# Feed-forward output projections as seven half-size products, with weight sums by accumulating DMAs, in a two-layer GLA and DeltaNet trunk

## The chip, the cores and the metric

The kernel runs on one core of one Trainium2 chip. The metric is the device time of one execution in microseconds (us); before the change it is 1276.69 us, the median of three runs (1276.61 to 1277.08). Engines are named as in the profile: PE is the tensor engine for matmuls, PEld its weight load, DVE the vector engine, ACT the scalar engine, POOL GpSimd, SP the engine that only issues DMAs. A DMA can be issued by SP or ACT through a hardware queue, or by POOL through a software queue.

## What is computed

The input x has 512 tokens of 1024 features in float32. Layer 0 mixes tokens with gated linear attention (GLA), layer 1 with gated DeltaNet (GDN). Each mixer and each feed-forward part is followed by a layer norm over the residual. Cut to what matters here:

```
def conv_ffn(x, w_in, conv_w, w_out):              # D_FF = 2816
    h = causal_dwconv(x @ w_in, conv_w)            # width 3, per channel
    gate, up = jnp.split(h, 2, axis=-1)
    return (jax.nn.gelu(gate, approximate=False) * up) @ w_out

for i in range(DEPTH):                             # DEPTH = 2
    y = gla_mixer(h, ...) if i % 3 == 0 else gdn_mixer(h, ...)
    h = layer_norm(ALPHA * h + y, ln_g[i, 0], ln_b[i, 0])
    h = layer_norm(ALPHA * h + conv_ffn(h, ...), ln_g[i, 1], ln_b[i, 1])
```

The change is in the last product of conv_ffn, (512 x 2816) times (2816 x 1024), once in each layer.

## The kernel before

**Precision.** Each float32 operand is split in two float32r parts, high and low: `split_out` (L450) lets ACT copy the source into the high part and DVE subtract it from the source for the low part. A product is three matmuls, high times high, high times low and low times high (`tm_terms`, L362, and `fm_mms`, L304).

**Two forms of product.** "fm" items (`fm_items`, L339) make 128 output features for all 512 tokens: the weights are held in the array, the tokens (`xh`, `xl`) stream, 8 blocks x 3 terms = 24 matmuls with 512 columns. "tm" products (`tm_half`, L367) make 128 tokens x 512 output columns: the activations are held and the weights stream.

**A feed-forward part** (`ffn`, L719) handles its 22 blocks of 128 inner features in two chunks of 12 and 10 (`CHUNKS`). For each block a gate item and an up item run; `ffn_conv` (L710) applies the three taps (one ACT pass, two DVE passes), ACT the GELU, DVE the product with the gate, and `split_out` makes `gh` and `gl`. Then `out_proj` (L403) multiplies the chunk with its rows of w_out: two column halves x four token blocks, each summed in a bank of PSUM over the chunk, then added to the residual h by DVE (L412 for the first chunk, L414 after it). In the last chunk the last four pairs of weight blocks (`TAIL`) are held in slots and the token blocks are finished one after another, with bn_stats (L419) and the layer norm spawned for each: `ln` (L606) between layers, which also makes the next `xh` and `xl` through PE transposes, or `ln_out` (L652) at the end, which stores the result. After a norm the first four fm items (`HEADSTART`) run first for tokens 0 to 255, then for 256 to 511, so that they begin before the last two blocks are normalised.

**Weights.** All weight tiles stand in one plan in the order of use. `issue` (L221) reads a tile of 512 KB by a DMA on SP into one of three raw buffers (`RAWB`) and splits it into one of four pairs of buffers (`WB`); `prefetch` (L285) issues up to `look` tiles ahead, 2 as a rule, while fewer than four are held. 

**Order.** Instructions are recorded by Python code that keeps a planned clock (`clk`) and runs side tasks as generators (`spawn`, `pump`); a scheduler then sets the final order on each engine. Every engine and every queue works through its own order, and a waiting instruction holds those behind it. Semaphores order the engines among each other.

**Memory.** All working tiles of 128 x 512 float32 come from one pool of 53 slots (`SLOTS`), the residual h among them. After the first feed-forward part h is written to DRAM by POOL's DMAs (`hd`) and read back after the GDN core (`unspill`, L671).

Of the kernel before, what the change touches and what calls it, by code (L numbers as in the profile page):

```python
# [25 lines left out]
ALPHA = 4.0 ** 0.25  # L26
LN_EPS = 1e-5
# [3 lines left out]
CHUNKS = ((0, 12), (12, 22))  # L31
SLOTS = 53
# [16 lines left out]
def blk(i, n=P):  # L49
    return slice(i * n, i * n + n)  # L50


class Trunk:
# [3 lines left out]
    def __init__(self, ctx, tc):  # L57
        self.tc = tc
        self.nc = nc = tc.nc
        self.n = 0  # L60
        ec = ctx.enter_context
        ap = ec(tc.tile_pool(name="acts", bufs=1))
        self.xh = ap.tile([P, NC, S], F32R, name="xh", tag="xh")
        self.xl = ap.tile([P, NC, S], F32R, name="xl", tag="xl")
        self.wp = ec(tc.tile_pool(name="wts", bufs=WB))
        self.mp = ec(tc.tile_pool(name="mem", bufs=SLOTS))
# [4 lines left out]
        self.dp = ec(tc.tile_pool(name="scratch", bufs=1, space=bass.MemoryType.DRAM))  # L71
        self.ident = self.keep([P, P], "ident")
# [5 lines left out]
        self.reset = self.keep([P, S], "reset")  # L78
        nc.vector.memset(self.reset, 1.0)
        nc.vector.memset(c4(self.reset)[:, :, 0:1], 0.0)  # L80
        self.h = None
        self.plan = []
        self.issued = 0
        self.taken = 0
# [12 lines left out]
        self.late = []  # L97
        self.first = None
        self.between = None
# [5 lines left out]

    def slot(self, s, dt=F32):
        return self.mp.tile([P, S], dt, name=self.uid(s), tag="slot")
# [4 lines left out]
    def small(self, shape, s, dt=F32, bufs=None):  # L112
        return self.sp.tile(shape, dt, name=self.uid(s), tag=s, bufs=bufs)

# [41 lines left out]
    def mm(self, out, a, b, start=True, stop=True):  # L156
# [4 lines left out]
        t = self.nc.tensor.matmul(out, a, b, start=start, stop=stop)  # L161
# [54 lines left out]

    @staticmethod
    def in_slots(item):
        return item[0] == "tm" and item[5]

    def issue(self, item):  # L221

        nc = self.nc
        if item[0] == "rep":
            return self.issue_rep(*item[1:])
        raw = self.rp.tile([P, 1024], F32, name=self.uid("raw"), tag="raw")
# [57 lines left out]

    def prefetch(self):  # L285
        while self.issued < min(len(self.plan), self.taken + self.look):
            item = self.plan[self.issued]
# [3 lines left out]
            self.issued += 1  # L291

# [46 lines left out]
    def fm_items(self, items):  # L339

        start = 0 if all(self.is_set(("x", tb)) for tb in range(NTB)) else HEADSTART
        first = items[:start]
        ws, banks = [], []
        for half in range(2 if first else 0):
            self.wait(("x", 2 * half), ("x", 2 * half + 1))
            for i, f in enumerate(first):
                if not half:
                    ws.append(self.weight())
                    banks.append(self.psum("fm"))
                self.fm_mms(banks[i], ws[i], half * 256, half * 256 + 256, self.pin and not half and i < 2)  # L350
                if half:
# [10 lines left out]
    def tm_terms(self, ps, ah, al, wh, wl, first, last):  # L362
        self.mm(ps, ah, wh, first, False)
        self.mm(ps, ah, wl, False, False)
        self.mm(ps, al, wh, False, last)
# [137 lines left out]
    def load_x(self, x):  # L503

        nc = self.nc
        self.h = [[self.slot("h") for _ in range(2)] for _ in range(NTB)]
# [99 lines left out]
    def ln(self, tb, spill=False):  # L606
# [36 lines left out]
        yield from self.until(("x", NTB - 1))  # L643
# [8 lines left out]
    def ln_out(self, tb, out):  # L652
        nc = self.nc
        gb, h = self.ln_gb(), self.h[tb]

        def center(mv):
            for hf in range(2):
                nc.vector.scalar_tensor_tensor(h[hf], h[hf], mv[:, 0:1], gb[hf], ALU.subtract, ALU.mult)

        mv, rs = self.ln_stats(tb, center)  # L660
        for hf in range(2):
            m = 2 if tb == NTB - 1 and hf else 1
            for i in range(m):
                cols = blk(i, S // m)
                nc.vector.scalar_tensor_tensor(h[hf][:, cols], h[hf][:, cols], rs, gb[2 + hf][:, cols],
                                               ALU.mult, ALU.add)
                (nc.sync, nc.scalar)[i].dma_start(out[blk(tb), hf * S + cols.start:hf * S + cols.stop],
                                                  h[hf][:, cols])
        yield 0.0

    def unspill(self, gb_rows):  # L671
# [4 lines left out]
        for hf in range(2):  # L676
            for tb in range(NTB):
                t = self.slot("h")
                nc.gpsimd.dma_start(t, self.hd[blk(tb), blk(hf, S)])
# [16 lines left out]
    def ffn_plan(self, w_in, w_out):  # L696
        for f0, f1 in CHUNKS:
# [3 lines left out]
            self.plan_out(w_out, f0 * P, f1 - f0, TAIL if f1 == NF else 0)  # L701
# [8 lines left out]
    def ffn_conv(self, ps, cw, b):  # L710
        nc = self.nc
        a = self.slot("conv")
# [6 lines left out]
    def ffn(self, cw, li, g, b, final, out=False):  # L719
        nc = self.nc  # L720
        for ci, (f0, f1) in enumerate(CHUNKS):
            gs, act, items = [], {}, []
            for f in range(f0, f1):
                def gate(ps, f=f):
                    a = self.ffn_conv(ps, cw, f)
# [3 lines left out]
                def up(ps, f=f):  # L729
                    u = self.ffn_conv(ps, cw, NF + f)  # L730
                    nc.vector.tensor_mul(u, u, act.pop(f))  # L731
                    t = self.slot("gh", F32R), self.slot("gl", F32R)
                    self.split_out(*t, u)
                    gs.append(t)
# [3 lines left out]
            last = ci == len(CHUNKS) - 1  # L738
# [5 lines left out]
            a = lambda c, tb: (gs[c][0][:, blk(tb)], gs[c][1][:, blk(tb)])  # L744
            self.out_proj(a, f1 - f0, ci == 0, final if last else None, 2 if last and out else 1)
# [38 lines left out]
    def gla_consts(self, w_gk2, b_gk, norm_w):  # L784
        nc = self.nc

        self.gk2 = self.keep([96, S], "gk2", F32R)
# [13 lines left out]
        self.gla_nw = self.keep([P, 256], "gla_nw")  # L801
# [8 lines left out]
        self.gla_mask = self.keep([P, S], "gla_mask", U8)  # L810
        nc.gpsimd.tensor_copy(self.gla_mask, mk)
        self.b_gk = self.keep([P, 4], "gla_b")
        self.spawn(self.columns([(b_gk.rearrange("(n p) -> n p", p=P), 4, self.b_gk)]), 12.0)

    def gla(self, li, g, b):
# [83 lines left out]
        ss = self.keep([P, GH, 4], "gla_ss")  # L899
        rr = self.keep([P, GH, 4], "gla_rr")  # L900
# [89 lines left out]
    def mixer_out(self, y, li, g, b, final=None):  # L990
# [7 lines left out]
        self.out_proj(a, NC, True, self.ln)  # L998

# [24 lines left out]
    def gdn_conv(self, ps, b):  # L1024

        nc = self.nc
        a = self.slot("conv")
# [8 lines left out]
    def gdn(self, li, g, b):  # L1036
        nc = self.nc
        self.flags = {f: t for f, t in self.flags.items() if f[0] in ("x", "h")}
        hs = slice(H0, H0 + 8)
        al = self.gdn_al  # L1040
        spilled = self.gb_rows
        keep = lambda s: self.keep([P, DH, 4], s)
        eb, neb, ebl, cd = (keep(s) for s in ("gd_eb", "gd_neb", "gd_ebl", "gd_cd"))
        bn, bp, rk = keep("gd_bn"), keep("gd_bp"), keep("gd_rk")
        ssq, rr = self.keep([P, 2, DH, 4], "gd_ssq"), self.keep([P, DH, 4], "gd_rr")
        bt = self.keep([P, 4, 64], "gd_bt")
# [7 lines left out]
        def ba_done(ps):  # L1054
# [8 lines left out]
            ea = self.keep([P, 1], "gd_ea")  # L1063
# [50 lines left out]
        def k_done(ps, hd):  # L1114
            k[hd] = self.gdn_conv(ps, 8 + hd)
# [4 lines left out]
        def q_done(ps, hd):  # L1120
            q[hd] = self.gdn_conv(ps, hd)
# [134 lines left out]
        def v_done(ps, hd):  # L1256
            vc[hd % 2] = self.gdn_conv(ps, 16 + hd)
# [145 lines left out]
def kernel(  # L1403
# [41 lines left out]
    t.drain()  # L1445

# [28 lines left out]
```

## Time and profile before

| | |
|---|---|
| median of three runs | 1276.69 us |
| span of the profiled execution, first to last instruction | 1274.8 us |
| time around the span, the difference of the two | 1.9 us |
| granted PE clock over the span | 0.999 |
| DMA queue of SP and its like (q1): moved, share of 16 engines | 116.28 MB, 31.1% |
| DMA queue of POOL (q0): moved, share of 16 engines | 8.50 MB, 2.3% |

The profiled execution is given by its span; its own time from launch to end isn't shown apart, so the runs' median is taken for it. In a row of instruction groups stand line, engine, operation, out<-in, shapes and count, then busy us and mean ns of one, then the idle time before them and who ended it. Busy times of one engine can overlap a little, since a matmul starts before the one ahead of it has drained. In a row of waits stand the waiting engine and line, the releaser, then us in total, times and the longest. In a piece of the chain or of the timeline stand start and length in us, engine, line and count. In a stretch, busy us and count of each engine are followed by the granted clock, the share of the 16 DMA engines that is busy, and GB/s.

### The profile page before, as it was taken

How to read it: one execution, taken by the hardware profiler on the slowest of the kernel's cores; microseconds unless marked ns; L12 is line 12 of the kernel's file. 1: busy time of each engine (PE TensorE's matmuls, PEld its weight loads, DVE VectorE, ACT ScalarE, POOL GpSimd, SP SyncE). 2: the span in 40 equal slices, each digit the busy share in tenths (PEclk: the TensorE clock that was granted, in tenths of full speed). 3: DMA queues.
4: the chain of work that ended last, by engine and by line, in shares of the span. 5: the costliest groups of instructions: out<-in, count | busy, mean ns of one | idle time of the engine just before them, and what ended most of it. 6: DMA issues, size and time to landing. Idle time of an engine off the chain costs nothing.

```text
span 1274.8 us, 17225 instructions
## 1 busy us (share of the span) xinstructions
PE 1260.9 (99%) x6682; PEld 1068.4 (84%) x6682; DVE 785.5 (62%) x1383; ACT 552.2 (43%) x1042; POOL 112.5 (9%) x152
## 2 busy tenths in 40 slices
PE   8999999999999999999999999999999999999997
PEld 8878888988888888889888888988988888888886
DVE  4953556676643466555789955679587653366656
ACT  4644444544421244435765544543644431244430
POOL 4000000070000000001023120100053000000000
PEclk9999999999999999999999999999999999999999
DMA  7322224143333333351354431234053333333331
GB/s 207 112 70 63 67 93 123 50 132 99 99 99 99 99 92 92 98 151 66 103 149 113 122 75 51 68 116 137 17 152 101 94 96 99 99 99 99 94 105 66
DMA packets 167234, 126.53 MB, mean 99 GB/s; under 512 B 16104, under 2 KB 139818, under 8 KB 167152
## 3 DMA queue, kind: packets, MB, share of 16 engines
q1 hardware_dynamic: 162064, 116.28, 31.1%
q0 software_dynamic: 3888, 8.50, 2.3%
q8 instruction: 52, 0.85, 0.3%
q10 hardware_dynamic: 1200, 0.66, 0.2%
q14 instruction: 30, 0.25, 0.1%
HBM read 119.63 MB, written 5.78 MB: 98 GB/s over the span
## 4 chain that ended last, share of the span: by engine, by line
PE 94%; DVE 3%; ACT 1%; DMA 1%; issue 1%; SPq 0%; DVEq 0%; ACTq 0%
PE fm L161 50%; PE tm L161 35%; PE o L161 2%; PE xT L178 1%; PE R L161 1%; PE V L161 1%; DVE wl L451 1%; PE qkT L178 1%; PE vn L161 1%; PE pq L161 1%; PE pg L161 1%; PE yT L178 1%; PE s L161 0%; DMA h<-in_x_dram 0%; PE qs L161 0%
## 5 line engine op out<-in xcount | busy, mean ns | idle before, releaser
L451 DVE TENSOR_TENSOR wl<-raw,wh 128x1024 fp32r<-128x1024 f32 (+1 forms) x190 | 237.8, 1253 | 312.2 <-ACT wh L451 312.0
L161 PE MATMUL fm<-xh,wh 128*128 128x512 f32 (+2 forms) x1104 | 402.6, 367 | 0.7 <-ACT xh L451 0.7
L161 PE MATMUL fm<-xl,wh 128*128 128x512 f32 (+2 forms) x1104 | 399.9, 365 | 0.0
L161 PE MATMUL fm<-xh,wl 128*128 128x512 f32 (+1 forms) x1088 | 396.0, 366 | 0.0
L451 ACT CAST wh<-raw 128x1024 fp32r<-128x1024 f32 (+1 forms) x190 | 199.0, 1047 | 279.4 <-PE tm L161 166.8
L161 PEld LDWEIGHTS fm<-xh,wh 128*128 128x128 f32 (+1 forms) x1104 | 206.9, 188 | 33.7 <-ACT xh L451 0.9
L161 PEld LDWEIGHTS fm<-xl,wh 128*128 128x128 f32 (+1 forms) x1104 | 207.0, 188 | 32.4
L161 PEld LDWEIGHTS fm<-xh,wl 128*128 128x128 f32 x1088 | 204.2, 189 | 33.5
L716 DVE SCALAR_TENSOR_TENSOR conv<-fm,ffn_cw,conv 128x511 f32<-128x511 f32 (+1 forms) x176 | 130.8, 746 | 3.0
L161 PE MATMUL tm<-wl,gh 128*128 128x512 f32 x290 | 112.4, 388 | 0.0
L161 PE MATMUL tm<-wh,gl 128*128 128x512 f32 x290 | 112.4, 388 | 0.0
L161 PE MATMUL tm<-wh,gh 128*128 128x512 f32 x290 | 112.4, 388 | 0.0
L451 ACT CAST gh<-conv 128x512 fp32r<-128x512 f32 x44 | 27.3, 621 | 124.2 <-DVE conv L731 124.1
L161 PE MATMUL tm<-wh,xh 128*128 128x512 f32 x192 | 78.5, 409 | 0.8 <-ACT qk L836 0.8
L161 PE MATMUL tm<-wh,xl 128*128 128x512 f32 x192 | 75.2, 392 | 0.0
L161 PE MATMUL tm<-wl,xh 128*128 128x512 f32 x192 | 75.0, 390 | 0.0
L726 ACT ACTIVATE conv<-conv 128x512 f32<-128x512 f32 x44 | 27.8, 632 | 94.8 <-DVE conv L716 94.8
L161 PEld LDWEIGHTS tm<-wh,gl 128*128 128x128 f32 x290 | 54.4, 188 | 11.2
L161 PEld LDWEIGHTS tm<-wl,gh 128*128 128x128 f32 x290 | 54.4, 188 | 11.2
L161 PEld LDWEIGHTS tm<-wh,gh 128*128 128x128 f32 x290 | 54.4, 188 | 11.1
L714 ACT ACTIVATE conv<-fm,ffn_cw 128x512 f32<-128x512 f32 x88 | 60.0, 682 | 0.2
L647 POOL TENSOR_TENSOR h<-h,gb 128x512 f32<-128x512 f32 x16 | 27.1, 1716 | 344.3 <-DMA gb<-in_ln_g_dram 235.8
(280 smaller groups left out, 1556.5 us busy)
## 6 DMA issues: line engine op xcount, KB each, us to landing
raw<-in_ffn_w_in_dram SPq DMA_DIRECT2D x88, 512.0 KB, 3.8
raw<-in_ffn_w_out_dram SPq DMA_DIRECT2D x44, 512.0 KB, 3.8
raw<-in_gdn_w_in_dram SPq DMA_DIRECT2D x32, 512.0 KB, 4.0
raw<-in_gla_w_in_dram SPq DMA_DIRECT2D x23, 512.0 KB, 3.6
raw<-in_gla_w_out_dram SPq DMA_DIRECT2D x8, 512.0 KB, 3.7
raw<-in_gdn_w_out_dram SPq DMA_DIRECT2D x8, 512.0 KB, 3.8
h<-in_x_dram SPq DMA_DIRECT2D x8, 256.0 KB, 4.3
hd<-h POOLq DMA_DIRECT2D x8, 256.0 KB, 2.5
```

Of the source, the lines that this page charges most:

```text
L161: t = self.nc.tensor.matmul(out, a, b, start=start, stop=stop)
L178: t = self.nc.tensor.transpose(out, a, self.ident[:n, :n])
L451: return self.nc.scalar.copy(dst_h, src), self.nc.vector.tensor_sub(dst_l, src, dst_h)
L647: nc.gpsimd.tensor_mul(h[hf], h[hf], gb[hf])
L714: nc.scalar.activation(a, ps, AF.Identity, scale=tap(2))
L716: nc.vector.scalar_tensor_tensor(a[:, d:], ps[:, :S - d], tap(2 - d), a[:, d:], ALU.mult, ALU.add)
L726: nc.scalar.activation(a, a, AF.Gelu)
```

## The change

**Seven products.** With tokens in halves 1 and 2, pairs of inner feature blocks (even, odd) and output columns in halves, the output product is a 2 x 2 block product. In place of eight half-size products it is made of seven. `folded` replaces `out_proj` for the feed-forward parts; the mixers keep `out_proj`.

```
+FORMS = ("a11", "a22", "a12", "w1", "v2", "v3", "v4")
+FOLD = (("b11", "a11", 0), ("b21", "a12", 1), ("t1", "w1", 2), ("t2", "v2", 0), ("b22", "v4", 2), ("t3", "v3", 0),
+        ("t4", "a22", 0))
+NEXT = {"b11": "b12", "t1": "b22", "t2": "b21"}
-CHUNKS = ((0, 12), (12, 22))
-SLOTS = 53
+GROUPS = ((0, 8), (8, 16), (16, 22))
+SLOTS = 45
+FFN_SLOTS = 6
+FOLDED = 2
+PASSING = 4
+AHEAD = 2
```

Each entry of FOLD is a product: a weight quarter or sum, an activation form, and one of three pairs of PSUM banks. Products that share a pair go on summing in the same banks, and after each of them DVE adds or subtracts the banks' present value to one or another block of h:

```
+        banks = [[self.psum("fold") for _ in range(2)] for _ in range(3)]
...
+            at, op = {"b11": (top, ALU.add), "t1": (high, ALU.add), "t2": (right, ALU.subtract), "b21": (top, ALU.add),
+                      "t3": (high, ALU.subtract), "b22": (right, ALU.add), "t4": (low, ALU.add)}[name]
...
+        for name, form, at in FOLD:
+            f = FORMS.index(form) * 256
+            for i in range(0, m, 2):
+                w = self.weight()
+                n = min(2, m - i)
+                for r in range(2):
+                    ps = banks[at][r]
+                    for j in range(n):
+                        _, fh, fl = forms[i + j]
...
+                        self.tm_terms(ps, fh[:, cols], fl[:, cols], *w[j], begin, end, True)
+                    if i + 2 >= m:
+                        update(name, r, ps)
```

Here m is the number of pairs in a group, 4, 4 and 3; top and right are token blocks 2 and 3, high and low are blocks 0 and 1. A weight tile holds the quarters of two pairs (one in the last tile of a group of 3 pairs).

**Activation forms.** The up product of the even and the odd block of a pair is written into one tile; DVE makes four more 256-column parts, and `split_out` makes 1792 columns at once (in parts for the last pair of a group):

```
+                    nc.vector.tensor_sub(part(4), part(0), part(2))
+                    nc.vector.tensor_sub(part(5), part(4), part(1))
+                    nc.vector.tensor_sub(part(6), part(1), part(0))
+                    nc.vector.tensor_add(part(7), part(5), part(3))
```

**Weight sums.** Quarters b11, b21, b22 and b12 are read by SP into tiles of their own (`sum`, 2 buffers, and `pass`, 4 buffers), up to `AHEAD` beyond the prefetch. b11 becomes t1 = b11+b12, then t2 = t1+b22, then t4 = t2+b21 in place, and the tile of t3 is b12+b22. Each sum is an accumulating DMA on POOL's queue, recorded right after the split of the former value:

```
+        if add:
+            self.nc.gpsimd.dma_start(dst, src, accum_op=ALU.add)
+        else:
+            self.nc.sync.dma_start(dst, src)
...
+        self.fold_read(group, {"t3": "b12"}.get(name, name), i, t)
+        if name == "t3":
+            self.fold_read(group, "b22", i, t, True)
...
+        self.split_out(wh[:, cols], wl[:, cols], t[:, cols])
+        self.vec(0.62 * n)
+        if name in NEXT:
+            self.fold_read(group, NEXT[name], i, t, True)
```

In a fold `look` is 3 in place of 2.

**Pools by stage.** `stage` releases the pool of working tiles and opens a new one for the GLA mixer (45 slots), the first feed-forward part (6 slots beside the tiles above), the GDN mixer and the second feed-forward part. Constants of one mixer move from the constant pool into the stage's pool (`own`), the scan mask `reset` is set anew for the GDN mixer, and h gets a pool of 8 tiles of its own, which the GDN mixer uses for its eight k tiles while h is in DRAM.

**Ends.** In the last group h is complete first for token blocks 2 and 3, then for 0 and 1, and the norms are spawned in that order. The first fm items after it run for tokens 256 to 511 first:

```
+        self.halves = (0, 1)
-        for half in range(2 if first else 0):
+        for turn, half in enumerate(self.halves if first else ()):
...
+        if last:
+            self.halves = (1, 0)
```

In `ln_out` the last store that is cut in two is that of token block 1 in place of block 3.

More of the change, by code (lines that the diff above doesn't have):

```diff
@@ L83, in __init__ @@
         self.issued = 0
+        self.loaded = 0
         self.taken = 0
@@ L104, in uid, with stage, resets, resid @@
         return f"{s}_{self.n}"
+    def stage(self, name, slots):
+        if self.mp is not None:
+            self.mp.release()
+        self.mp = self.tc.alloc_tile_pool(name=name, bufs=slots, reuse_waits="tile")
+    def resets(self):
+        self.reset = self.own([P, S], "reset")
+        self.nc.vector.memset(self.reset, 1.0)
+        self.nc.vector.memset(c4(self.reset)[:, :, 0:1], 0.0)
+    def resid(self, s):
+        return self.hp.tile([P, S], F32, name=self.uid(s), tag="h")
     def slot(self, s, dt=F32):
@@ L160, in mm @@
         self.clk += n * (0.00045 if b.dtype == F32R else 0.00175)
-        t = self.nc.tensor.matmul(out, a, b, start=start, stop=stop)
+        t = self.nc.tensor.matmul(out, a, b, start=start, stop=stop, skip_group_check=joined)
         if self.pin:
@@ L215, in plan_out, with plan_fold @@
                 self.plan_tm(w, row + 2 * cp * P, min(2, n - 2 * cp), hf * S, hf == 1 and cp >= npair - tail)
+    def plan_fold(self, w, f0, f1):
+        group = {"w": w, "f0": f0, "m": (f1 - f0) // 2}
+        for name, _, _ in FOLD:
+            for i in range(0, group["m"], 2):
+                self.plan.append(("fold", group, name, i))
     @staticmethod
@@ L291, in prefetch, with load_ahead @@
             self.issued += 1
+        self.load_ahead(self.taken + self.look + AHEAD)
+    def load_ahead(self, until):
+        self.loaded = max(self.loaded, self.issued)
+        while self.loaded < min(len(self.plan), until) and self.plan[self.loaded][0] == "fold":
+            self.fold_load(*self.plan[self.loaded][1:])
+            self.loaded += 1
     def weight(self):
@@ L642, in ln @@
             return
-        yield from self.until(("x", NTB - 1))
+        for i in range(NTB):
+            yield from self.until(("x", i))
         yield RESID_DELAY + 10.0 * tb
@@ L661, in ln_out @@
         for hf in range(2):
-            m = 2 if tb == NTB - 1 and hf else 1
+            m = 2 if tb == 1 and hf else 1
             for i in range(m):
@@ L785, in gla_consts @@
         nc = self.nc
-        self.gk2 = self.keep([96, S], "gk2", F32R)
+        self.gk2 = self.own([96, S], "gk2", F32R)
         def factor():
@@ L800, in gla_consts @@
         self.spawn(factor(), 3.0)
-        self.gla_nw = self.keep([P, 256], "gla_nw")
+        self.gla_nw = self.own([P, 256], "gla_nw")
         self.late.append((self.gla_nw, norm_w))
```

167 lines of the change are left out of this document (125 added, 42 removed).

## The prediction

> **What bounds the kernel now.** I read the page first (busy shares, then the chain that ended last), then what the tensor engine waited for, then stretches.
>
> ```profile
> span 1274.8 us, 17225 instructions
> PE 1260.9 (99%) x6682; PEld 1068.4 (84%) x6682; DVE 785.5 (62%) x1383; ACT 552.2 (43%) x1042; POOL 112.5 (9%) x152
> PE 94%; DVE 3%; ACT 1%; DMA 1%; issue 1%; SPq 0%; DVEq 0%; ACTq 0%
> ```
> ```profile
> PE xT L178 <- DVE ln_mv L592: 1.0, 1, 1.0
> ```
> ```profile
> 1037.75 65.28 PE tm L161 x288
> 1103.03 108.80 PE fm L161 x480
> 1211.83 54.82 PE tm L161 x270
> ```
> ```profile
> core 0: us, PE busy (x) PEld busy (x) DVE busy (x) ACT busy (x) POOL busy (x), PEclk, DMA share, GB/s
> 300.00:365.00 65.00, 65.00 (x288) 53.84 (x287) 40.06 (x49) 26.73 (x37) 0.00 (x0) 1.00 0.33 98
> 370.00:424.00 54.00, 54.00 (x240) 44.69 (x239) 16.71 (x17) 10.55 (x10) 0.00 (x0) 1.00 0.32 95
> ```
>
> The chain is 94% PE, and PE is never held at a layer norm for more than the 1.0 us shown. The three chain pieces are the second feed-forward layer from its first output product on; PE runs through them without a gap. So a matmul that goes is time saved, unless PE begins to wait. One 128x512 matmul costs 65.28/288 = 0.2267 us (a row of its own says 0.39 because neighbours overlap). The stretches show the room beside PE at full clock: DVE is busy 62% while the up-projections run and 31% during the output product; the DMA engines are busy 0.32 at 95 GB/s, so all 16 together move 297 GB/s, and a 512 KB weight tile is 1.77 us of their time.
>
> **The saving.** An output projection has 22 feature blocks x 4 token blocks x 2 column halves x 3 terms = 528 matmuls. Seven products of 11 pairs x 2 token blocks x 3 terms make 462. Two layers: 132 x 0.2267 = **29.9 us**.
>
> **What is added beside PE.** Each product has its own split weights: 7 x 11 half tiles per layer are 38.5 splits for 22, 33 more in all.
>
> ```profile
> L451 DVE TENSOR_TENSOR wl<-raw,wh 128x1024 fp32r<-128x1024 f32 x188 | 236.5, 1259 | 312.2 <-ACT wh L451 312.0
> L716 DVE SCALAR_TENSOR_TENSOR conv<-fm,ffn_cw,conv 128x510 f32<-128x510 f32 x88 | 65.7, 749 | 3.0
> L731 DVE TENSOR_TENSOR conv<-conv,conv 128x512 f32<-128x512 f32 x44 | 33.6, 763 | 1.6
> L253 DVE TENSOR_TENSOR wsl<-raw,wsh 128x512 fp32r<-128x512 f32 x32 | 21.1, 690 | 8.3 <-ACT wsh L252 8.3
> L414 DVE TENSOR_TENSOR h<-h,tm 128x512 f32<-128x512 f32 x15 | 10.2, 685 | 18.9 <-PE tm L161 18.9
> L451 ACT CAST wh<-raw 128x1024 fp32r<-128x1024 f32 x188 | 197.7, 1052 | 279.4 <-PE tm L161 166.8 <-PE fm L161 96.8 <-DMA raw<-in_ffn_w_in_dram 7.2
> L252 ACT CAST wsh<-raw 128x512 fp32r<-128x512 f32 x32 | 18.3, 626 | 13.6 <-DMA raw<-in_ffn_w_out_dram 7.7 <-DMA raw<-in_gdn_w_out_dram 3.9 <-DMA raw<-in_gla_w_out_dram 2.0
> ```
>
> DVE gains 33 x 1.26 = 42 us of splits, 52 more updates of h (32 before, 84 after) at 0.69 = 36, and per pair about 2.3 us of token sums and wider splits = 51 (by size from the rows above). In the up-projections that lifts 62% to some 72%; in a product of 4 pairs (24 matmuls, 5.44 us) DVE does two splits and two updates, 3.9 us, also 72%. I cost this at nothing: its cover is PE work of the same stage. If the cover is gone it shows at the two places below. Pools by stage, h in a pool of its own, the mask set anew and the reversed halves add under 1 us of DVE or ACT work behind running matmuls: nothing.
>
> **The waits it adds.** Sums of quarters grow in one tile: b11, then +b12 (t1), +b22 (t2), +b21 (t4), each after the split of the former value. t2 directly follows t1, so that sum is the tight one. The tile t3 = b12+b22 is read by SP and also summed by POOL, and in the order that the changed program has on POOL its two transfers stand *ahead* of the sums for t2.
>
> ```profile
> raw<-in_ffn_w_out_dram SPq DMA_DIRECT2D x44, 512.0 KB, 3.8
> h<-hd POOLq DMA_DIRECT2D x8, 256.0 KB, 3.6
> ```
> ```profile
> L679 POOL DMA_DIRECT2D h<-hd x8 | 4.3, 543 | 46.9 <-PE o L161 42.4 <-ACT vn L1353 3.6 <-PE vn L161 0.8
> ```
>
> Let E be the DMA time of one accumulating 512 KB, with 0 at the first product matmul. With four weight buffers b21's second tile is split from 0 on: 1.05 + 1.26 = 2.3. That frees its buffer for t3's second read: 3.8, so 6.1. POOL issues its sum (0.54, 6.65), then t2's, both on one queue: 2E, then what a landing takes beyond the engines' time, 3.8 - 1.77 = 2.0, then cast 1.05 and subtraction 1.26, the latter needed one matmul (0.23) later: 10.7 + 2E. t2 starts at 3 x 5.44 = 16.3. PE stalls 2E - 5.6 there, and at t2's second tile E - 2.72 more (one sum behind per 12 matmuls), each only if positive. Behind the waiting split DVE holds t2's second split, b22's splits and t1's update, ACT the casts of the same tiles; all are due only when t2 is done.
>
> With 3 pairs products last 4.08 us and t2 starts at 12.2. Here DVE is what is late: b21's half split (0.63 + 0.69), two taps 1.49, product 0.76, token sum 0.42, update 0.69, split 0.69, sum 0.42, t1's split 1.26 end at 7.0; issue 0.54, E, 2.0, 1.05, 1.03: 11.65 + E. PE stalls E - 0.6.
>
> No row shows an accumulating transfer. Lower bound: it costs what a plain one does, E = 1.77. Upper bound by rows: three plain transfers one after another (source in, destination out, result back), 3 x 1.77 = 5.3. A plain transfer reads once and writes once, this one reads source and destination and writes: 3 passes for 2, **E = 2.65**, nearer to the plain row since writing isn't doubled. Then: four groups of 4 pairs 0, two of 3 pairs 2.1 each, **4.2 us**. At 1.77 it is 2.4; at 5.3, 4 x (5.0 + 2.6) + 2 x 4.7 = 40.
>
> The Trainium skill, *Collectives: The Full Stack* (The bandwidth ceiling: the fold count and why AG ≠ RS ≠ AR), speaks against the change: an add on the way costs because two sources are read, measured ratio 1.93. By it E would be 3.4, an estimate from that page, and the sum about no change. No run so far shows such a transfer.
>
> **The two ends.** The last group's products finish token blocks 2 and 3 after b22, two products (8.2 us) before the end, but blocks 0 and 1 only with t4. Before, one block ended every 5.4 us. The update after t3 must read its bank before t4 may write it, and in DVE's order it stands behind the norms.
>
> ```profile
> 577.93 0.68 DVE L414 TENSOR_TENSOR h<-h,tm 128x512 f32<-128x512 f32 x1
> 578.53 0.68 DVE L633 TENSOR_TENSOR xl<-xf,xh 128x512 fp32r<-128x512 f32 x1
> ```
> ```profile
> 5.23 1.19 PE L178 MATMUL xT<-ident,h 128*128 128x128 f32 x8
> ```
> ```profile
> 1266.36 0.28 PE L161 MATMUL tm<-wsh,gl 128*128 128x256 f32 x1
> 1266.67 0.42 DVE L414 TENSOR_TENSOR h<-h,tm 128x256 f32<-128x256 f32 x1 [0.21 <-PE tm L161]
> 1267.59 0.24 DVE L592 BATCH_NORM_AGGREGATE ln_mv<-ln_st 128x2 f32<-128x18 f32 x1
> 1267.86 0.15 DVE L596 TENSOR_SCALAR ln_var<-ln_mv 128x1 f32<-128x1 f32 x1
> 1267.93 1.40 DVE L658 SCALAR_TENSOR_TENSOR h<-h,ln_mv,gb 128x512 f32<-128x512 f32 x2
> 1269.26 0.15 DVE L600 RECIPROCAL ln_rs<-ln_root 128x1 f32<-128x1 f32 x1
> 1269.45 0.22 DVE L601 SCALAR_TENSOR_TENSOR ln_t<-ln_rs,ln_var 128x1 f32<-128x1 f32 x1
> 1269.70 0.16 DVE L602 SCALAR_TENSOR_TENSOR ln_rs<-ln_t,ln_rs 128x1 f32<-128x1 f32 x1
> 1271.47 0.37 ACTq L667 DMA_DIRECT2D out_dram<-h  x1
> ```
>
> *Into the GDN layer.* From b22's end to x for blocks 2 and 3, DVE has thirteen 512-wide operations (0.60 apart), four splits of 1.26 and one of 0.6, two chains of small ones of 1.1, two scalings 0.54 and two casts 0.43: 17.5 us. PE has t3, t4 and 16 transposes: 8.2 + 2.4 = 10.6. It waits up to 6.9; at least 4 if two of the next weights' splits find gaps. I take **5.5**.
>
> *At the end of the kernel.* From b22's end DVE has six updates and six statistics (0.60, each pair 0.12 more: 7.9), two splits 1.95, four chains of small ones (0.9), four pairs of centring 1.40 and of scaling 1.42: 24.7 us. The last store takes 3.3 (1271.47 to 1274.8). So the end is 24.7 - 8.2 + 3.3 = 19.8 after the matmuls would have ended, where it was 8.2 (1266.6 to 1274.8): 11.6 lost at most, 7 if DVE catches up before t3 ends. I take **10.5**.
>
> **Sum.** -29.9 + 4.2 + 5.5 + 10.5 = -9.7. The span of 1274.8 has 1.9 us around it to the median of 1276.69, which I keep: **1267**.
>
> **Rivals.**
> 1. *An accumulating transfer costs two plain ones*, E = 3.53. For it: it moves the destination too. Stalls 4 x (1.5 + 0.8) + 2 x 2.9 = 15; -29.9 + 15 + 16 = +1: 1278.
> 2. *The sums are late throughout: slower.* One mechanism, the queue of POOL's sums ahead of t2. All stalls together are 14E - 34.5; with 16 for the ends the change loses from E = 3.46 on, 1.95 plain ones. At 5.3: 40 + 16 - 29.9 = +26, 1303. For it: up to four sums queue in a row and nothing else can run them; against: two thirds of the DMA engines' time is free.
> 3. *The ends are hidden* as they are now (no wait above 1.0 us): -29.9 + 4.2, 1251. Against: DVE's 17.5 us for PE's 10.6.
> 4. *The saving doesn't come*: DVE at 72% delays the up-projections, which then give it back: 1277 or more. Against: PE has never waited there.
>
> **How the numbers follow.** Forecast 0.38, rival 1 0.22 (0.02 faster, 0.10 the same, 0.10 slower), rival 2 0.30, rival 3 0.05, rival 4 0.05 (slower). 0.2%, 2.6 us, is what I take as told apart. Faster 0.38 + 0.02 + 0.05 = 0.45, same 0.10, slower 0.45. The forecast's own range is 1260 (E plain, ends 4 and 7) to 1272 (E = 3.1). The range reaches 1258 to 1299, where E is 5.0: it leaves out rival 3 and the worse half of rival 2.
>
> **What would show it.** Right: 924 products of 0.227; gaps before t2 of about 2 us in groups of 3 pairs alone; about 5 us of PE waiting before the GDN layer; over 12 us from the last matmul to the end, or DVE waits before t4. Wrong: gaps at t2 in all six groups (E above 2.8), named as waits for the accumulating DMA through ACT; or no gaps and 132 matmuls' worth not gained.

## The result and the profile after

The changed kernel takes 1283.4 us (1282.05 to 1286.6 in 4 runs), 1.0054 times the time before (95% interval 1.0042 to 1.0067): 6.7 us slower, where 9.7 faster was forecast. Its profiled execution has a span of 1280.3 us, 5.5 more than the one before. The first fence has its page, in the order of the lines shown of before; the second is what the tensor engine waited for: in total, times, the longest.

```profile
span 1280.3 us, 17262 instructions
PE 1245.8 (97%) x6520; PEld 1044.6 (82%) x6520; DVE 908.6 (71%) x1545; ACT 595.3 (46%) x1064; POOL 171.1 (13%) x200
PE 78%; DVE 11%; DMA 5%; ACT 3%; issue 2%; POOL 0%; SPq 0%; DVEq 0%; ACTq 0%; POOLq 0%
```
```profile
PE fold L188 <- ACT wh L538: 5.6, 4, 2.3
PE fold L188 <- DVE wl L538: 4.5, 6, 0.8
PE fm L188 <- DVE xh L716: 1.9, 1, 1.9
PE fold L188 <- DVE ln_rs L689: 1.8, 1, 1.8
PE xT L205 <- DVE h L703: 1.8, 1, 1.8
PE fold L188 <- DVE h L881: 1.7, 1, 1.7
```

PE was 94% of the chain that ended last and is 78% now. The first two rows are t2 waiting for a split of its sum, in all six groups; the others are the two ends. But PE's busy time fell by only 15.1 us where 132 matmuls are 29.9, so what PE does has become slower as well. Two views show it: pieces of the chain (start, length, what), and stretches with the granted clock.

```profile
334.07 16.82 PE fold L188 x71
```
```profile
585.15:588.56 3.41, 1.50 (x7) 0.90 (x6) 3.27 (x6) 3.41 (x10) 2.23 (x4) 1.00 0.42 60
588.56:591.98 3.42, 2.92 (x13) 2.62 (x14) 3.32 (x10) 1.99 (x4) 0.00 (x0) 0.50 0.60 155
591.98:595.39 3.41, 3.41 (x18) 3.41 (x18) 3.13 (x13) 1.72 (x3) 1.07 (x2) 0.50 0.23 77
```

71 products from 334.07 on take 16.82 us: without the first step of 0.34 and the length of the last, 0.40, that is 0.233 for each of 69 steps; the timeline has 0.2333, from the first product of every group on, ahead of any wait and at full clock. Before it was 0.2267. Around 588 us, at the start of the GDN layer, PE stands still for 2.4 us in two waits, and from 588.56 to 595.39 it runs at a granted clock of 0.50. (Where an expectation below says 0.57, that is the mean of a stretch that begins at full clock.) The same happens in the last group of the second layer (start, length of one, idle time before it and what ended it):

```profile
1244.89 0.51 PE L188 MATMUL fold<-wh,fh 128*128 128x512 f32 x1 [2.34 <-ACT wh L538]
1246.15 0.50 PE L188 MATMUL fold<-wl,fh 128*128 128x512 f32 x1 [0.75 <-DVE wl L538]
1246.49 0.39 PE L188 MATMUL fold<-wh,fl 128*128 128x512 f32 x1
...
1247.90 0.63 PE L188 MATMUL fold<-wl,fh 128*128 128x512 f32 x1
1248.33 0.63 PE L188 MATMUL fold<-wh,fl 128*128 128x512 f32 x1
```

These are the first matmuls of t2: 2.34 us for the cast of the late sum, 0.75 for its subtraction, and a little later eight matmuls that start 0.43 us apart, which costs 1.6.

The price that the prediction had no row for stands in the table of DMA queues (packets, MB, share of the time of 16 engines); q0 is POOL's queue, before, after, and with its median time to landing.

```profile
q0 software_dynamic: 3888, 8.50, 2.3%
```
```profile
q0 software_dynamic: 15920, 31.57, 13.3%
...
sum<-in_ffn_w_out_dram POOLq DMA_DIRECT2D x30, 512.0 KB, 5.9
```

The 44 accumulating transfers' worth of 512 KB (40 whole ones and 8 halves) took 13.3% of 1280.3 less 2.3% of 1274.8, 141 us: E = 3.2 us each, 1.8 times the plain 1.77. They land 5.9 us after their issue.

### The profile page after: what moved, and what is told of

Its sections match the earlier page's. It is cut to its first block, busy times and chain, and to the rows that moved or that the text cites. A ratio compares the mean times of both kernels' runs of the same rounds, so it can differ in the third digit from the quotient of the medians.

```text
span 1280.3 us, 17262 instructions
## 1 busy us (share of the span) xinstructions
PE 1245.8 (97%) x6520; PEld 1044.6 (82%) x6520; DVE 908.6 (71%) x1545; ACT 595.3 (46%) x1064; POOL 171.1 (13%) x200
## 3 DMA queue, kind: packets, MB, share of 16 engines
q0 software_dynamic: 15920, 31.57, 13.3%
## 4 chain that ended last, share of the span: by engine, by line
PE 78%; DVE 11%; DMA 5%; ACT 3%; issue 2%; POOL 0%; SPq 0%; DVEq 0%; ACTq 0%; POOLq 0%
PE fm L188 43%; PE tm L188 17%; PE fold L188 9%; DMA sum<-in_ffn_w_out_dram 3%; DVE wl L538 3%; ACT wh L538 2%; PE o L188 2%; DMA pass<-in_ffn_w_out_dram 1%; DVE form L803 1%; DVE conv L803 1%; PE xT L205 1%; DVE fl L538 1%; PE R L188 1%; DVE form L826 1%; PE V L188 1%
## 5 line engine op out<-in xcount | busy, mean ns | idle before, releaser
L538 DVE TENSOR_TENSOR wl<-raw,wh 128x1024 fp32r<-128x1024 f32 (+1 forms) x154 | 193.3, 1257 | 187.6 <-ACT wh L538 187.2
L188 PE MATMUL fold<-wh,fh 128*128 128x512 f32 x308 | 123.3, 400 | 9.2 <-ACT wh L538 5.6
L188 PE MATMUL fold<-wl,fh 128*128 128x512 f32 x308 | 123.0, 399 | 4.5 <-DVE wl L538 4.5
L188 PE MATMUL fold<-wh,fl 128*128 128x512 f32 x308 | 122.3, 397 | 0.0
L538 ACT CAST wh<-sum 128x1024 fp32r<-128x1024 f32 (+1 forms) x48 | 47.0, 979 | 96.1 <-DMA sum<-in_ffn_w_out_dram 34.8
L538 DVE TENSOR_TENSOR wl<-sum,wh 128x1024 fp32r<-128x1024 f32 (+1 forms) x48 | 54.2, 1130 | 37.4 <-ACT wh L538 37.3
L188 PEld LDWEIGHTS fold<-wh,fh 128*128 128x128 f32 x308 | 58.1, 189 | 26.1 <-ACT wh L538 7.6
L188 PEld LDWEIGHTS fold<-wl,fh 128*128 128x128 f32 x308 | 58.3, 189 | 20.2 <-DVE wl L538 6.6
L188 PEld LDWEIGHTS fold<-wh,fl 128*128 128x128 f32 x308 | 58.3, 189 | 13.8
L803 DVE SCALAR_TENSOR_TENSOR form<-fm,ffn_cw,form 128x511 f32<-128x511 f32 x88 | 65.7, 746 | 2.4 <-ACT form L801 0.8
```

Of the source, the lines that this page charges most:

```text
L188: t = self.nc.tensor.matmul(out, a, b, start=start, stop=stop, skip_group_check=joined)
L538: return self.nc.scalar.copy(dst_h, src), self.nc.vector.tensor_sub(dst_l, src, dst_h)
L803: nc.vector.scalar_tensor_tensor(a[:, d:], ps[:, :S - d], tap(2 - d), a[:, d:], ALU.mult, ALU.add)
```

## The experiments

Times are medians, ratios are against runs of the kernel before on the same chip.

**1. Where the tiles lie (e1_shift, e2_before_shift).** The pools by stage moved every tile of the feed-forward layers. In the built program the stationary tiles of the products begin at 32 past a multiple of 64 bytes, the weight buffers on a multiple of 64; before, both did.

```
+        self.pad = self.cp.tile([P, 8], F32, name="pad", tag="pad")   # e1: after, last tile of the pool const
+        self.pad = self.qp.tile([P, 8], F32, name="pad", tag="pad")   # e2: before, in a pool of its own ahead of "mem"
```

> The changed kernel with 32 bytes of padding ahead of its pools by stage, nothing else. Theory (where the tiles lie): the products' 512-wide matmuls start 0.2333 us apart instead of 0.2267 because their stationary operand begins 32 bytes past a multiple of 64 while the moving one begins on one; with both on a multiple of 64 all 924 products and the 192 of the GLA output projection that showed it are back at 0.2267. 1116 x 0.0067 = 7.4 us of matmul time; what lies ahead of t2 in a group is only waited for longer, so 4 to 5 us of it are gained: 1279. Rival (the products are slow for what they are, by their order over banks or by the granted clock): they stay at 0.2333 and the time at 1283.

> The kernel before with 32 bytes of padding ahead of its pool of slots, nothing else. Theory (where the tiles lie): the 1050 output-projection matmuls whose stationary operand lies in a slot and whose moving one lies in the weight buffers go from 0.2267 to 0.2333 us; nothing waits in this kernel, so all of it shows: +7.0 us, 1283.7. Rival (the slow matmuls belong to Strassen's products): no change, 1276.7.

e2 takes 1283.82 us, ratio 1.0056 (1.0043 to 1.0069): 7.1 us slower for 32 bytes, as expected, in a kernel that computes the same and has one small memset of the padding more. e1 takes 1283.28 us, no change from 1283.4, and its products are as slow as they were. The chain of e2, the product that took 65.28 us before; and of e1, the piece that took 16.82 after:

```profile
1042.01 67.19 PE tm L164 x288
```
```profile
334.66 16.83 PE fold L190 x71
```

67.19/288 = 0.2333. So the place of an operand sets the step, but not by multiples of 64. (The 192 other slow matmuls are 96 each in the output projections of the GLA and the GDN layer.)

Is it the place of the stationary tile itself, or its distance from the moving one? At the end of a layer's output product the last weights lie in slots too (`wsh`, `wsl`), so that in e2 both tiles of a matmul moved by 32 bytes. Two stretches of equal length in e2, PE alone, the first with weights from the weight buffers, the second with weights from slots:

```profile
1230.00:1243.60 13.60, 13.60 (x60) 1.00 0.21 68
1252.90:1266.50 13.60, 13.60 (x62) 1.00 0.10 39
```

The timeline has steps of 0.2333 in the first and of 0.2267 in the second. So it is the distance that counts.

**2. Which distance counts (e5_shift224, e8_before_shift128).** In all fast pairs of tiles, in both kernels, the distance between the moving and the stationary tile is a multiple of 512 bytes. In the changed kernel it is 288 more than one, in e1 320, in e2 32.

```
+        self.pad = self.cp.tile([P, 56], F32, name="pad", tag="pad")   # e5: 224 bytes, distance 0
+        self.pad = self.qp.tile([P, 32], F32, name="pad", tag="pad")   # e8: 128 bytes, distance 128
```

> The changed kernel with 224 bytes of padding in place of 32. With 32 bytes both operands began on a multiple of 64 and the products stayed at 0.2333 us, so the theory is put anew: a matmul is slow when its two operands begin at different places within a larger stretch; in every pair of tiles that ran at 0.2267 the two addresses differ by a multiple of 512. With 224 bytes they do so for the products too. Theory: all 924 at 0.2267, 4 to 5 us gained where nothing waits for a sum: 1279. Rival (the products are slow for what they are): 0.2333, 1283.

> The kernel before with 128 bytes of padding ahead of its slots in place of the 32 that cost 7.1 us. Theory A (what counts is where the operands lie within 128 bytes): no change, 1276.7. Theory B (it is 256 or 512 bytes): the 1050 matmuls are slow again, 1283.8.

```profile
334.03 16.39 PE fold L190 x71
```
```profile
1040.87 66.93 PE tm L164 x288
```

With a distance of 0 the piece takes 16.39 us (the first fence, e5): the products are back at 0.2267. With 128 (the second, e8) a matmul takes 0.2324, and e8 takes 1282.83 us, ratio 1.0044 (1.0031 to 1.0057). So 128 bytes is not the stretch that counts; 256 was not tried apart from 512. The theory of the matmuls holds, but e5's time does not move: 1283.71 us. What the matmuls save ahead of t2 lengthens the wait at t2, and the clock fell after t2 in five groups of six where it had fallen in one, with a mean of 0.986 over the profiled run. That run is the slowest of e5's six (1280.03 to 1286.51), and in the profiled run of e1, whose products are as slow as those of the changed kernel, the clock fell in four groups: how often it falls changes from run to run, so its share in e5's time is not shown.

**3. What the add costs (e3_plain).**

```
-            self.nc.gpsimd.dma_start(dst, src, accum_op=ALU.add)
+            self.nc.gpsimd.dma_start(dst, src)
```

> The changed kernel with plain DMAs in place of the accumulating ones, on the same queue, in the same order and of the same size; each sum is left out, a tile then holds the quarter read last. Theory (the add on the way is what is late, 3.2 us of the DMA engines for 512 KB against 1.77): the time of the accumulating queue falls by nearly half, the gaps before t2 go in the groups of 4 pairs and shrink to some 1 us in those of 3, together 14.5 to about 3 us: 1272. Rival (POOL's issue and its queue are late, whatever the transfer does): gaps and time stay, 1283.

```profile
q0 software_dynamic: 10288, 31.57, 7.8%
...
sum<-in_ffn_w_out_dram POOLq DMA_DIRECT2D x30, 512.0 KB, 4.0
```

1268.8 us, ratio 0.994 (0.9928 to 0.9952), 14.6 under the changed kernel. The queue moves the same 31.57 MB; its share falls from 13.3% to 7.8%, which by the same sum is 1.58 us for 512 KB: accumulating costs 2.0 times as much on the same queue. The gaps in groups of 4 pairs are gone, those of 3 pairs keep 0.75 us of waiting. The add makes the sums late: each transfer takes 1.6 us less of the DMA engines without it. POOL's issue of one fell as well, from 1.20 to 0.72 us; the run does not separate this smaller part.

**4. Another product between t1 and t2 (e4_swap), inconclusive.**

```
-        ... ("t1", "w1", 2), ("t2", "v2", 0), ("b22", "v4", 2), ("t3", "v3", 0), ...
+        ... ("t1", "w1", 2), ("b22", "v4", 2), ("t2", "v2", 0), ("t3", "v3", 0), ...
```

> The changed kernel with the product b22 taken ahead of t2 in each group; the sums in the banks allow it. Theory (the sum of t2 is late by 1 to 3.5 us and everything else has room): the sum gets one more product of 4 to 5.4 us, the gaps before t2 go, 1 to 3 us of waits may come back at t4, whose sum now has one product less: 1271. Rival (the queue of sums is too long in all, not late at one place): the gaps move on to t2 or t4 and the time stays within 3 us of 1283.

1295.39 us, 12 slower than the changed kernel. It did not test what it was for: the scheduler put the first two matmuls of t2 ahead of b22's on PE, so PE still waited at the same place and b22 was held behind it. Its trace shows the queue, though (POOL's issues in the second group of the second layer, then ACT's cast for t2):

```profile
1128.52 1.20 POOL L333 DMA_DIRECT2D pass<-in_ffn_w_out_dram  x1 [8.33 <-DMA pass<-in_ffn_w_out_dram]
1136.41 1.20 POOL L333 DMA_DIRECT2D pass<-in_ffn_w_out_dram  x1 [6.68 <-DMA pass<-in_ffn_w_out_dram]
1137.14 2.95 POOL L333 DMA_DIRECT2D sum<-in_ffn_w_out_dram  x2
```
```profile
1147.89 1.04 ACT L538 CAST wh<-sum 128x1024 fp32r<-128x1024 f32 x1 [8.09 <-DMA sum<-in_ffn_w_out_dram]
```

`pass` is t3's tile here: POOL waits for its plain read, issues its two sums, and only then the two for t2. ACT has nothing to cast for 8.1 us until the first of those lands. Why this order cost 12 us more than the changed kernel's was not followed further.

**5. t2's sums first (e6_sums_first), and with the addresses (e7_both).** A plain change of program order would not do, since the scheduler orders POOL's queue too; the sums are kept in the order in which they are written, t4's are written later, and SP reads all quarters a step earlier.

```
-            self.nc.gpsimd.dma_start(dst, src, accum_op=ALU.add)
+            self.tc.keep_in_program_order(self.nc.gpsimd.dma_start(dst, src, accum_op=ALU.add))
-NEXT = {"b11": "b12", "t1": "b22", "t2": "b21"}
+NEXT = {"b11": ("b11", "b12"), "t1": ("b11", "b22"), "b22": ("b11", "b21")}   # tile to add to, quarter
-AHEAD = 2
+AHEAD = 3
...
```

> The changed kernel with the accumulating DMAs kept in an order on POOL: both sums for t2, then t3's first, t4's first, t3's second, t4's second; before, t3's two stood ahead of t2's. The products keep their order. Theory (t2's sum is late because it queues behind t3's): no gap before t2 in the groups of 4 pairs, some 1 us in those of 3, no new wait at t3 or t4; 14.5 us of gaps and slow clock become about 3: 1272. Rival (the queue of sums is too long in all): the waits come back at t3 and t4 and the time stays at 1280 or more.

> The order of sums of the run before and the 224 bytes together. Theory: with no sum late, what the matmuls save is no longer waited away; 7.4 us of the two groups of slow matmuls come off nearly whole: 1265 to 1266, under the kernel before. Rival (the sums are late by their own length): the faster matmuls only wait longer, 1270 or more.

POOL's issues in the second group of the first layer, in the changed kernel and in e6:

```profile
451.92 1.20 POOL L333 DMA_DIRECT2D pass<-in_ffn_w_out_dram  x1 [6.39 <-DVE form L838]
452.65 2.95 POOL L333 DMA_DIRECT2D sum<-in_ffn_w_out_dram  x2
```
```profile
448.14 1.20 POOL L333 DMA_DIRECT2D sum<-in_ffn_w_out_dram  x1 [12.98 <-DVE wl L538]
452.08 1.20 POOL L333 DMA_DIRECT2D sum<-in_ffn_w_out_dram  x1 [2.74 <-DVE wl L538]
452.81 1.71 POOL L333 DMA_DIRECT2D pass<-in_ffn_w_out_dram  x1
```

e6 takes 1276.93 us (ratio 1.0, 0.9991 to 1.0008), e7 1273.12 us (0.9968, 0.9955 to 0.998). In both, no group of 4 pairs has a gap at t2, and in three of e7's four the first 144 products run through in 32.64 us, 0.2267 each; in the fourth PE waits 1.3 us before t4 for DVE's update of h. So t2's sum was late because it stood behind t3's; rival 2's mechanism is shown, though the earlier reads came with the new order and were not tried apart. The place in the queue and the price of the add are both needed for it: with plain transfers in the old order (e3) the gaps in groups of 4 pairs are gone as well. The times are 5 and 7 us above what was expected, and e7's lies where its rival put it (1270 or more). The groups of 3 pairs keep 2.5 to 2.9 us of gaps, and in the last groups what is gained earlier is waited for at the end: in e7 PE waits 3.5 us for a norm before t4 where it was 1.8, and the clock falls there.

**6. Does the wait bring the clock down? (e10_fill).** On top of e5, matmuls that the result does not need keep PE busy between t1 and t2.

```
+                if name == "t2" and i == 0:
+                    spare = self.psum("spare")
+                    for k in range(8):
+                        t = self.nc.tensor.matmul(spare, forms[0][1][:, :P], forms[0][2][:, :S], start=True, stop=True)
...
```

> The changed kernel with 224 bytes and, in each group, 8 matmuls into a spare bank between t1 and t2 (1.8 us of TensorE work that the result doesn't need). Theory (the clock falls to 0.57 because PE stands still for some 2.7 us or more of a short stretch): with the idle time cut to under 2 us the matmuls after t2 start at full clock in all groups; the five falls after t2 in the run with 224 bytes alone cost 9 us, and the sums' own lateness stays: 1275. Rival (the clock falls for another reason): the slow stretches stay and the time is 1283 or more, by up to 11 us more if the 48 extra matmuls don't fit the gaps.

The second group of the second layer in e5 and in e10:

```profile
1143.85 0.50 PE L190 MATMUL fold<-wh,fh 128*128 128x512 f32 x1 [2.40 <-ACT wh L540]
1145.11 0.50 PE L190 MATMUL fold<-wl,fh 128*128 128x512 f32 x1 [0.76 <-DVE wl L540]
...
1146.44 0.63 PE L190 MATMUL fold<-wh,fl 128*128 128x512 f32 x1
```
```profile
1140.12 1.98 PE L903 MATMUL spare<-fl,fh 128*128 128x512 f32 x8
1142.11 0.49 PE L190 MATMUL fold<-wh,fh 128*128 128x512 f32 x1
1143.37 0.50 PE L190 MATMUL fold<-wl,fh 128*128 128x512 f32 x1 [0.76 <-DVE wl L540]
1143.71 0.40 PE L190 MATMUL fold<-wh,fl 128*128 128x512 f32 x1
```

In e5 the matmuls after the wait start 0.43 us apart (1146.01, 1146.44, 1146.86); in e10 t2 starts no later in this group and runs at full clock. Of e5's five falls after t2 four are gone; the one in the group where PE still stood 1.8 and 0.8 us after the spare matmuls stayed. The time is 1280.91 us, ratio 1.0029 (1.0018 to 1.004), 2.8 under e5, where 9 were expected. The mechanism is shown, its worth was set too high: t2 came 1.1 and 2.2 us later in the first two groups than in e5, and two of the five falls lie in groups whose end DVE sets; which of these weighs more was not tried.

Why a wait of some 2 us brings the clock down in one group and not in another shows in the traces when they are divided at the times at which the clock changes. In each trace all these times lie whole multiples of 3.41 us apart. Two such stretches in the second group of the first layer of the changed kernel, whose wait of 2.05 us in all (1.30 and 0.75) did not bring the clock down, and two in the last group of e6, whose wait of 1.97 did (PE, PEld, DVE, ACT, POOL; the granted clock is the third number from the end):

```profile
458.85:462.27 3.42, 2.00 (x8) 1.06 (x6) 0.65 (x1) 1.04 (x1) 0.00 (x0) 1.00 1.07 194
462.27:465.68 3.41, 2.78 (x12) 2.18 (x12) 1.84 (x3) 2.35 (x3) 1.20 (x1) 1.00 0.12 22
```
```profile
1237.00:1240.42 3.42, 1.44 (x5) 0.81 (x5) 1.83 (x2) 1.44 (x2) 0.47 (x1) 1.00 1.06 163
1240.42:1243.83 3.41, 3.41 (x10) 2.63 (x9) 2.90 (x4) 1.69 (x3) 2.59 (x3) 0.50 0.83 145
```

In the first kernel the edge between two stretches parts the wait into 1.42 and 0.63 us; in e6 all of it lies in one stretch, and the next one runs at half the clock.

**7. The ends (e11_ends_old, e9_last_old).** The last group of each layer by the full product, as before; its tiles take the place of the folded ones.

```
-            self.plan_fold(w_out, f0, f1)
+            if f1 == NF:
+                self.plan_out(w_out, f0 * P, f1 - f0, (f1 - f0) // 2)
+            else:
+                self.plan_fold(w_out, f0, f1)
...
-            self.folded(forms, gi == 0, final if last else None)
+            if last:
+                self.out_proj(a, f1 - f0, False, final, 2 if out else 1)
+            else:
+                self.folded(forms, gi == 0, None)
```

> The changed kernel, its order of sums and its addresses as they are, with the last group of each layer computed as before. Theory (ends, t2 in groups of 3 pairs and late sums are losses of their own): 21.8 us saved by 96 fewer matmuls, 6.5 us of gaps at t2 in the four groups left, 5 to 6 us of slow matmuls there and in the GLA layer, 0 to 4 at the ends: 1267 to 1271, 12 to 16 under the changed kernel. Rival (the ends cost nothing of their own, what is lost there would be lost elsewhere): the 36 more matmuls make it slower, 1284 or more.

> The order of sums and the 224 bytes, and the last group of each layer (6 blocks) computed as before, by the full product with one token block finished after the other, over 3 pairs instead of 4. Theory (the last groups lose at their ends, where DVE is late, and at t2, where 3 pairs are too short for the sum): the four groups left save 96 matmuls, 21.8 us, no gap is left before t2, PE waits 1 to 2 us into the GDN layer and the end is at most some 4 us longer than before: 1255 to 1259. Rival (DVE's added work holds PE wherever it is put): the gain over the kernel with both mends stays below the 8.2 us that the 36 more matmuls cost: 1273 or more.

e11 takes 1274.64 us, ratio 0.9981 (0.9972 to 0.999): with 36 matmuls *more* it is 8.8 us faster than the changed kernel. So the two last groups lost 8.8 + 8.2 = 17 us by their form: ends, gaps at t2 and slow clock together. It is 3.6 us above the 1271 that was expected at most. e9, with the order and the padding as well, takes 1266.2 us, ratio 0.9916 (0.9902 to 0.993). No product waits in it, but it is 7 us or more above what was expected: its products step 0.2324 again, because the full product's small tiles moved the pools, and the distance is 128.

**8. With the right padding (e12_best).** 608 bytes in place of 224.

> The run with the last groups as before had its products at 0.2324 us again: its pools by stage began 128 bytes off a multiple of 512 from the weight buffers, because the full product brings other small tiles with it. Here the padding is 608 bytes, so that the difference is a multiple of 512. Theory: the 672 products, the 252 matmuls of the last groups that read the weight buffers and the 192 of the GLA layer come back to 0.2267; with the 0.0057 us that 128 bytes cost, 6 us of 1266.2, nothing else moves: 1260. Rival (waits take the gain, as they did in the changed kernel): 1264 or more.

The page of e12, what its PE waits for, and a group's products:

```profile
span 1259.0 us, 17249 instructions
PE 1241.7 (99%) x6574; PEld 1051.3 (84%) x6574; DVE 880.0 (70%) x1504; ACT 589.1 (47%) x1060; POOL 155.8 (12%) x184
```
```profile
PE fm L191 <- DVE xh L726: 1.7, 1, 1.7
PE tm L191 <- ACT qk L1033: 0.8, 1, 0.8
PE fm L191 <- DVE xl L730: 0.7, 1, 0.7
```
```profile
987.09 32.64 PE fold L191 x144
```

1260.75 us (1260.41 to 1261.38), ratio 0.9874 (0.9858 to 0.9891): 16.2 us under the kernel before, and 22.7 under the changed one. 96 fewer matmuls are 21.8 us; most of what is missing of it is the wait of 1.7 and 0.7 us into the GDN layer with the slow clock behind it, and an end 2 us longer.

## Why the prediction was wrong

Two steps failed. The larger is the term of 4.2 us for the waits at t2: they took 14.4, with the slow clock behind one of them. The other is the saving of 29.9 us, of which slower matmuls took back 7.5 that the prediction put at nothing.

**The saving: wrong.** 924 products were counted rightly, but priced at 0.2267. They took 0.2333, which is 6.2 us, and 192 matmuls of the other two output projections 1.3. The step that failed is the sentence that costs pools by stage "nothing": it counted instructions and not where the tiles would lie. No row of before could show it, since there all pairs lie a multiple of 512 bytes apart. e2, e8 and e5 show the cause: the distance between a matmul's two tiles.

**Waits at t2: the mechanism right, the size too small.** Gaps in all six groups, named as waits on the sum through ACT, is what the prediction gave as its sign of being wrong, with E above 2.8. E is 3.2 where 2.65 was taken. With 3.2 the prediction's own 14E - 34.5 gives 10.3 us for the 4.2; the gaps are 12.8 (steps of the timeline less 0.2333: 0.9, 2.6, 2.7, 1.9, 1.1, 3.6) and the slow clock behind the last of them 1.6. The count of passes (3 for 2) was the wrong guess. Two smaller terms of the same sum were mostly short as well: the plain read of t3's second tile, for which POOL waits ahead of t2's sums, was taken at 3.8 us and took 4.1, 5.6, 3.6 and 4.1 in the chain of the four groups of 4 pairs, and POOL's issue takes 1.20, not 0.54. The Trainium skill, *Collectives: The Full Stack* (The bandwidth ceiling: the fold count and why AG ≠ RS ≠ AR), prices an add on the way, in a reduce-scatter, at 1.93 by its two reads, which gave 3.4; the runs show 1.8 against SP's plain transfers and 2.0 on the same queue (e3), so it was nearer than the row. Of the rivals, rival 1 at 3.53 was nearest in E, and rival 2's queue is the mechanism (e6). That the change came out slower, as rival 2 had it, is in part luck: by its own sum, 14E - 34.5 and 16 for the ends, the kernel would still be 3.6 us faster at 3.2.

**The clock: not in the prediction.** It priced a stall at its own length. Twice the clock fell to 0.50 after one, which cost 1.6 and 2.3 us again.

**Into the GDN layer: the number right by luck.** 5.5 was forecast, all of it waiting. The waits are 1.76, 1.92 and 0.50, near the lower bound of 4, and 3.2 more than the 1.0 of before. 25 matmuls at 0.2133 in place of 0.12 add 2.3, which makes 5.5; but this part is the clock, which the forecast did not price.

**The end of the kernel: too high.** 10.5 was taken from 7 to 11.6. PE waits 1.8 and 1.7 before and in t4, and from the end of the last matmul to the end of the span it is 11.7 us instead of 8.2: 7.0. That is the lower bound in size, but not the case behind it: DVE had not caught up when t3 ended, since PE then waited 1.8 us for it (the row with `ln_rs`).

**DVE at nothing: right.** In an up-projection it is busy 72% (50.42 of the 70 us from 370 on), as forecast, and PE has no wait there; those of the changed kernel step 0.2267. Rival 4 is out, and so is rival 3.

Together: -29.9 + 7.5 + 14.4 + 5.5 + 7.0 = +4.5 for the 5.5 of the spans; the 1.0 left was not traced. Had E alone been right, the forecast would have been 1273; the matmuls and the clock, which it did not look for, make up the rest. (The upper end of the range, 1299 for E = 5.0, is 1298 by the prediction's own sum.)

The losses do not add up one by one: faster matmuls alone gave nothing (e5), where t2's sum set the time; sums in order alone gave 6.5 us (e6), then the matmuls 3.8 more (e7), and the ends with padding 12.4 (e12).

## What to carry to other kernels

When a change moves tiles, compare the distance between the moving and the stationary tile before and after, modulo 512 bytes, and look at the start-to-start step of the matmuls themselves: 0.2333 for 0.2267 hides in a PE that is 99% busy. A sum that is built by accumulating DMAs needs its place in the queue fixed by its due time, and is to be counted at twice a plain transfer (1.8 to 2.0 times here). In this kernel the seven products (Strassen's form) pay in the groups whose result nobody waits for; the last group is better left in the form that finishes one token block after the other (e11, e9).

## What the runs showed of the hardware

- **Distance of a matmul's operands.** A 128x512 fp32r matmul starts 0.2267 us after the one before it when its two tiles lie a multiple of 512 bytes apart, 0.2333 at 32, 288 and 320 bytes off and 0.2324 at 128. 256 was not tried. A matmul whose two tiles moved together by 32 bytes stayed at 0.2267 (e2).
- **Clock after a wait.** In each trace the granted clock changes only at times that lie whole multiples of 3.41 us apart, and between them it is 1.00 or 0.50. At t2 it depends on how long PE stands still within one such stretch. In the 46 groups of eight kernels (the changed one, e1, e3, e5, e6, e7, e10, e11) it never fell where no stretch held more than 1.47 us of idle time (32 groups), and always where one held 1.71 or more (14 groups). By the wait in all, from 2.0 to 2.4 us, it is down in some groups and not in others. Outside these groups the bound is less sharp: in e4 a stretch with 1.8 us and in e5, at the start of the GDN layer, one with 1.9 did not bring it down. The matmuls then step 0.427 us for one or two stretches. The Trainium skill, *TensorE: Matmul & The Clock Gate* (Part 1: The HAM clock gate), says that the clock is halved after an idle window of some 3.4 us and that this window runs free of the kernel; the trace agrees on its length, on its phase, which differs from run to run, and on the step, the 0.4267 us that the page gives for 512 columns at half the clock. The page asks for a whole idle window, and here 1.71 us of idle time in one were enough.
- **Issue and spread.** POOL takes 1.20 us to issue an accumulating DMA of 512 KB and 0.72 for the same one as a plain DMA (e3). Kernels in which PE waits for such sums in groups of 4 pairs spread over 4 to 7 us from run to run (e1: 1279.97 to 1287.04), e6 and e7, where it waits in groups of 3 alone, over 2, and e12, where it does not, over 1.
